# Opening of a transformer block: square sums on VectorE, wide row products, another order of products, zero products

## Chip, cores and metric

One core of a Trainium2 chip (trn2) runs the kernel; the other cores are idle. The metric is device time in microseconds (us) from one launch to its end; lower is better. Three runs of the kernel before took 1899.18, 1899.2 and 1902.77 us, median 1899.2.

## What is computed

One layer on 256 tokens of width 2048, all in float32: a feed-forward half step, attention of two kinds, a second feed-forward half step. Only the first lines matter here:

```
mod = silu(c) @ w_ada + b_ada                      # 9 vectors of 2048: shift, scale, gate, three times
sh1, sc1, gt1, sh2, sc2, gt2, sh3, sc3, gt3 = split(mod)
n   = modulate(rms_norm(h, g_ffn1), sh1, sc1)       # n * (1 + sc1) + sh1
f   = (silu(n @ w1_gate) * (n @ w1_up)) @ w1_down
h   = h + 0.5 * gt1 * f
```

`rms_norm` divides each token by the root of its mean square over the 2048 features.

## The kernel before

The features lie on the partitions: `h` is 16 tiles (`k` from 0 to 15) of 128 features x 256 tokens. A float32 product is made of three fast ones: the weights are split into a high half (`hiw`, cast by ScalarE, L84) and a low half (`low`, raw minus high, VectorE, L91), the normed tile into `nh` and its remainder `nl` (both in the tile `nx`); `mm3` (L225 to L227) adds `nh` by high, `nh` by low and `nl` by high. `Flow` streams the weights in units of 128x1024: `fetch` issues a load on SyncE's queue as soon as a low half has freed a raw buffer (4 of them), `to_hi` and `to_lo` make the halves, with 4 and 3 buffers, and `step` does so some units ahead of TensorE and also runs the jobs that make the shift, scale and gate vectors.

Such a vector entry is a row of 2048 weights times silu(c), summed. `cb` is silu(c) spread over all partitions (TensorE makes it with the matrix of ones into four banks `pc`, ScalarE copies it, L584). `ada_use` (L189) makes 128 entries at once on VectorE in two halves of 1024 columns (L198), each a multiply with a running sum and a read of the sum; the first half starts from a bias, the second from the first.

The opening, in the order written:

- SyncE loads the vectors, `x` in four quarters, two halves of the scale weights of k-tile 0, the shift weights of k-tile 0 (`wz`), then by turns two weight units and the scale and shift weights of k-tile 1 and of k-tile 2.
- TensorE is kept at work with products of zeros (`keep_busy`, L554; the zeros are tile 15 of `nx`): six at first, two after each of the first three quarters.
- For each quarter of `x`, ScalarE squares it (L583), VectorE adds the upper half of the features' tiles to the lower (L587), and TensorE sums over the partitions with two products with ones (L589) into `pstat`.
- The shift entries of k-tile 0 are made on TensorE instead of VectorE, as 16 products with one column, each in two passes (`pm`, L595). VectorE adds the bias (L601).
- `rstd_enter` turns `pstat` into the inverse root (`r1`) with one Newton step, and the scaled tile 0 (`g1`).
- `up_start` (L421) then runs over the first three k-tiles. `before1` (L610) prepares each: the four row halves on VectorE (scale, then shift; for k-tile 0 they are there already), the scaled tile (L321), `nh` on ScalarE (L324), high and low halves, `nl` (L327). For each k-tile there are 24 products of 512 columns, for two groups `G` of 4 banks, 12 each. They are called block 0, 1 and 2 here. All 8 banks (`pa`) hold their sums over the three blocks.
- From then on `up_pass` runs the same three k-tiles for the other groups (bank name `pu`), with units of 12 products, and so on to the end of the feed-forward part.

The order on each engine is the order written. At the end of the first feed-forward part and of the attention, `Stat.finish` (L300) sums the last squares over the partitions, again with zero-cost products of 128 columns (L305) before and behind the last one, 6 and 24, whose result nobody reads.

Of the kernel before, what the change touches and what calls it, by code (L numbers as in the profile page):

```python
# [15 lines left out]
P = 128  # L16
# [23 lines left out]
RATE_H = 0.5  # L40
QKV_ORDER = tuple((0, j, c) for c in range(8) for j in (2, 1)) + tuple(
    (g, j, c) for g in range(4) for j in (2, 1, 0) for c in range(8) if g or j == 0)
LOOK = 2
RAWW = 4
RAWA = 3
# [106 lines left out]
def build(tc, a):  # L152
    nc = tc.nc
    with ExitStack() as ctx:
# [5 lines left out]
        def bank(nm):  # L160
            return pb.tile([P, 512], F32, tag="b", name=nm)
# [27 lines left out]
        def ada_use(j, k, b, raw):  # L189
            if j in (1, 4, 7):  # L190
                scale, init = gsc[:, j // 3, k : k + 1], gin[:, j // 3, k : k + 1]
            elif j in (2, 8):
                scale, init = 0.25, gat[:, j // 3 // 2, k : k + 1]
            else:
                scale, init = 0.5, vec[:, BA + j * KT + k : BA + j * KT + k + 1]
            if b == 1:
                init = acc[:, j, k : k + 1]
            nc.vector.tensor_tensor_reduce(  # L198
                out=raw, in0=raw, in1=cb[:, b * CW : (b + 1) * CW], scale=scale, scalar=init,
                op0=ALU.mult, op1=ALU.add, accum_out=acc[:, j, k : k + 1])  # L200
            if b == 1:
                modded.add((j, k))
# [21 lines left out]
        def mm3(out, lh, ll, rh, rl, first, last, **kw):  # L224
            nc.tensor.matmul(out, lh, rh, start=first, stop=False, **kw)  # L225
            nc.tensor.matmul(out, lh, rl, start=False, stop=False, **kw)  # L226
            nc.tensor.matmul(out, ll, rh, start=False, stop=last, **kw)  # L227
# [14 lines left out]
        def rstd_tiles(w, tag):  # L242
            ts = [sp.tile([P, S], F32, tag="nt", bufs=4, name="rt")[:, :w] for i in range(2)]
            return ts + [(cp if w == 8 else sp).tile([P, w], F32, tag=tag, bufs=2, name=tag)]
# [13 lines left out]
        def rstd_enter(ps, n, k, jsc):  # L258

            t0, t1, r = ts = rstd_tiles(S, "rs")  # L260
            g = sp.tile([P, S], F32, tag="nt", bufs=4, name="nt")
            rstd_act(ps, n, ts)
            nc.scalar.activation(t0, r, AF.Square)
            nc.vector.tensor_scalar(t1, ps, -0.5 / n, -0.5 * EPS, ALU.mult, ALU.add)
            nc.vector.scalar_tensor_tensor(g, h[k], mod(jsc, k), r, ALU.mult, ALU.mult)
            nc.vector.tensor_tensor(t0, t0, t1, ALU.mult)
            nc.vector.scalar_tensor_tensor(g, t0, 1.5, g, ALU.add, ALU.mult)
            nc.vector.scalar_tensor_tensor(r, t0, 1.5, r, ALU.add, ALU.mult)
            return r, g

        class Stat:
# [28 lines left out]
            def finish(self, busy=None):  # L300
                def keep_busy(n):
                    if busy is not None:
                        idle = bank("idle")
                        for i in range(2 * n):
                            nc.tensor.matmul(idle[:, :P], busy[:, 0, :P], busy[:, 1, :P], start=True, stop=True)  # L305

                self.ps = bank("pstat")[:, :S]
                nc.tensor.matmul(self.ps, ones, self.acc, start=True, stop=False)
                keep_busy(3)
                nc.tensor.matmul(self.ps, ones, self.last, start=False, stop=True)  # L310
                keep_busy(12)
# [3 lines left out]
        def norm_parts(k, r, jsc, jsh, made=None):  # L315
            t = made if made is not None else sp.tile([P, S], F32, tag="nt", bufs=4, name="nt")
            sh = mod(jsh, k)

            def p0():
                if made is None:  # L320
                    nc.vector.scalar_tensor_tensor(t, h[k], mod(jsc, k), r, ALU.mult, ALU.mult)  # L321

            def p1():
                nc.scalar.activation(nh[k], t, AF.Identity, bias=sh)  # L324

            def p2():
                nc.vector.scalar_tensor_tensor(nl[k], t, sh, nh[k].bitcast(F32), ALU.add, ALU.subtract)  # L327
                normed.add(k)

            return p0, p1, p2  # L330
# [23 lines left out]
        def wide3(ps, k, whi, wlo, first, last):  # L354
            assert k in normed, k
            for t in range(2):
                ts_ = slice(t * P, (t + 1) * P)
                mm3(ps[t], nh[k][:, ts_], nl[k][:, ts_], whi, wlo, first, last)

        def keep(hp, G, j, ps):  # L360
            if j == 0:
# [23 lines left out]
        def hid_soon(hp, G, d):  # L385
# [32 lines left out]
            fl.at(d + 3, e2)  # L418
            fl.at(d + 4, e3)

        def up_start(hp, K, before):  # L421
            pa = [[[bank(f"pa{G}") for t in range(2)] for j in range(2)] for G in range(2)]
            for k in range(K):
                for G in range(2):
                    whi, wlo = before(k, G)
                    for j in range(2):
                        sl = slice(j * 512, (j + 1) * 512)
                        wide3(pa[G][j], k, whi[:, sl], wlo[:, sl], k == 0, k == K - 1)
                    if k == K - 1:
                        for j in range(2):  # L430
                            fl.at(0, lambda G=G, j=j: keep(hp, G, j, pa[G][j]))
# [96 lines left out]
        def big(nm):  # L528
            return hp.tile([P, 8, S], F32, tag="hid", name=nm)

        def eighths(nm):
            t = big(nm)
            return [t[:, 4 * b : 4 * b + 4, :].rearrange("p a s -> p (a s)") for b in range(2)]

        nc.sync.dma_start(vec, a["vecs"])
        for q in range(4):
            nc.sync.dma_start(h4[q], a["x"][q])
        zero, early = eighths("wz"), {}
        early[0, 1] = eighths("ra")
        for b in range(2):  # L540
            nc.sync.dma_start(early[0, 1][b], a["w_ada"][KT, b])
        for b in range(2):
            nc.sync.dma_start(zero[b], a["w_zero"][b])
        fl.fetch(1)
        for k in range(1, K1):
            for j in (1, 0):
                early[k, j] = eighths("ra")
                for b in range(2):
                    nc.sync.dma_start(early[k, j][b], a["w_ada"][j * KT + k, b])
            fl.fetch(min(2 * k + 1, RAWW - 1))  # L550

        idle = bank("idle")

        def keep_busy(n):  # L554
            for i in range(n):
                nc.tensor.matmul(
                    idle, nx[KT - 1][:, 0, :P], nx[KT - 1].rearrange("p t s -> p (t s)"), start=True, stop=True)

        cc = vec[:, CC : CC + KT]
        sc2 = cp.tile([P, KT], F32, name="sc2")  # L560
# [18 lines left out]
        for q in range(4):  # L579
            if q % 2 == 0:  # L580
                sq8 = big("sq1")
            sq = sq8[:, 4 * (q % 2) : 4 * (q % 2) + 4, :]
            nc.scalar.activation(sq, h4[q], AF.Square)  # L583
            nc.scalar.copy(cb[:, q * 512 : (q + 1) * 512], pcs[q])  # L584
            if q == 3:
                ada_use(1, 0, 0, early[0, 1][0])
            nc.vector.tensor_tensor(sq[:, 0:2, :], sq[:, 0:2, :], sq[:, 2:4, :], ALU.add)  # L587
            for i in range(2):
                nc.tensor.matmul(ps1, ones, sq[:, i, :], start=q + i == 0, stop=q + i == 4)  # L589
            if q < 3:  # L590
                keep_busy(2)
        ada_use(1, 0, 1, early[0, 1][1])
        pm = bank("pm")
        for c in range(KT):
            nc.tensor.matmul(  # L595
                pm[:, 0:1], zero[c // 8][:, c % 8 * P : (c % 8 + 1) * P], sc2[:, c : c + 1],
                start=c == 0, stop=c == KT - 1)
        r1, g1 = rstd_enter(ps1, D, 0, 1)

        def shift0():  # L600
            nc.vector.tensor_scalar(  # L601
                acc[:, 0, 0:1], pm[:, 0:1], 0.5, vec[:, BA : BA + 1], ALU.mult, ALU.add)

        modded.add((0, 0))

        mod_jobs(range(K1, KT), 1, 0, r1)
        ada_jobs([(j, k) for j in (2, 4, 3, 5) for k in range(KT)])
        mod_jobs(range(SPLIT2[0]), 7, 6)

        def before1(k, j):  # L610
            u = fl.u
            if j == 0:
                if k:
                    for i in (1, 0):
                        for b in range(2):
                            ada_use(i, k, b, early[k, i][b])
                fl.to_hi(u)
                p0, p1, p2 = norm_parts(k, r1, 1, 0, None if k else g1)
                p0()
                if k == 0:  # L620
                    shift0()
                p1()
                fl.to_hi(u + 1)
                fl.to_lo(u)
                p2()
                fl.to_lo(u + 1)
                if k == K1 - 1:
                    fl.top_up()
            if k == K1 - 1:
                return fl.step()  # L630
            fl.u += 1
            return fl.hi.pop(u), fl.lo.pop(u)

        up_start(hp, K1, before1)
        fl.pace(RATE_A)
        up_pass(hp, 2, 0, K1, "first")
        fl.pace(RATE_B)
# [406 lines left out]
```

## Time and profile before

| | us |
|---|---|
| median of 3 runs | 1899.2 |
| lowest, highest run | 1899.18, 1902.77 |
| the profiled execution | 1901.4 |
| its span, from the first to the last instruction | 1899.6 |
| TensorE busy in it | 1889.2 |
| VectorE busy in it | 1519.2 |
| ScalarE busy in it | 907.3 |
| mean share of the granted TensorE clock | 0.997 |

The profiled execution is one more run. All times of rows are us from the start of its span. "PE" is TensorE, "PEld" its weight loads, "DVE" VectorE, "ACT" ScalarE. A row of the timeline has the start, the time, engine, line, operation, `out<-in`, shapes, the count, and in brackets how long the engine was idle before and who released it. Matmuls overlap, so their step from start to start is shorter than the time of one.

### The profile page before, as it was taken

To read this page: it belongs to the slowest core of one execution; us is meant where nothing else is said; L and a number is where in the kernel's file an instruction comes from. 1 tells how busy PE (TensorE), PEld (TensorE's weight loads), DVE (VectorE), ACT (ScalarE), POOL (GpSimd) and SP (SyncE) were. 2 spreads that over 40 slices of the span, in tenths; PEclk is the share of its full clock that TensorE was granted. 3 is DMA by queue.
4 is the path that set the end of the run, shared out by engine and by line. 5 is a ranking of instruction groups with operands and counts; after the bars stand their busy time and mean duration, and the time that the engine had idled before them with its cause. 6 is when DMAs were issued, how large, how long until landed. Compare 5 with 4: busy or idle time off the path is not lost.

```text
span 1899.6 us, 25193 instructions
## 1 busy us (share of the span) xinstructions
PE 1889.2 (99%) x9136; PEld 1590.6 (84%) x9136; DVE 1519.2 (80%) x2058; ACT 907.3 (48%) x1261; POOL 1.2 (0%) x7
## 2 busy tenths in 40 slices
PE   8999999999999999999999999999999999999999
PEld 6888888888888888888888998888888888888888
DVE  7989988888889889788887988777877888866444
ACT  5654444444444443556556554654443544433442
POOL 0000000000000000000000000000000000000000
PEclk8999999999999999999999999999999999999999
DMA  8998987777799999586766546988888666687664
GB/s 343 363 336 309 308 294 251 249 257 248 254 365 359 350 367 351 198 265 231 258 220 225 185 152 221 311 307 277 269 274 266 217 227 217 222 288 244 201 198 132
DMA packets 140813, 503.85 MB, mean 265 GB/s; under 512 B 15632, under 2 KB 17936, under 8 KB 140688
## 3 DMA queue, kind: packets, MB, share of 16 engines
q1 hardware_dynamic: 140688, 502.25, 76.9%
q8 instruction: 71, 1.16, 0.2%
q14 instruction: 54, 0.44, 0.1%
HBM read 500.09 MB, written 2.10 MB: 264 GB/s over the span
## 4 chain that ended last, share of the span: by engine, by line
PE 98%; DVE 1%; issue 0%; ACT 0%; DVEq 0%
PE pu L227 16%; PE pu L226 16%; PE pu L225 16%; PE pd L225 6%; PE pd L227 6%; PE pd L226 6%; PE pd L230 4%; PE pd L231 2%; PE pso L225 2%; PE pso L226 2%; PE pso L227 2%; PE pqk L225 2%; PE pqv L225 2%; PE pqq L225 2%; PE pqk L226 2%; PE pqk L227 2%
## 5 line engine op out<-in xcount | busy, mean ns | idle before, releaser
L84 ACT CAST hiw<-rw 128x1024 fp32r<-128x1024 f32 x656 | 691.4, 1055 | 932.9 <-PE pu L227 441.6
L91 DVE TENSOR_TENSOR low<-rw,hiw 128x1024 fp32r<-128x1024 f32 x656 | 801.7, 1222 | 333.6 <-issue 109.9
L225 PE MATMUL pu<-hiw,nx 128*128 128x512 f32 x1352 | 527.7, 390 | 0.0
L227 PE MATMUL pu<-hiw,nx 128*128 128x512 f32 x1352 | 526.1, 389 | 0.0
L226 PE MATMUL pu<-low,nx 128*128 128x512 f32 x1352 | 526.0, 389 | 0.0
L227 PEld LDWEIGHTS pu<-hiw,nx 128*128 128x128 f32 x1352 | 253.8, 188 | 52.6
L226 PEld LDWEIGHTS pu<-low,nx 128*128 128x128 f32 x1352 | 253.8, 188 | 52.3
L225 PEld LDWEIGHTS pu<-hiw,nx 128*128 128x128 f32 x1352 | 253.8, 188 | 52.0
L225 PE MATMUL pd<-hiw,hd 128*128 128x512 f32 x528 | 205.9, 390 | 0.0
L227 PE MATMUL pd<-hiw,hd 128*128 128x512 f32 x528 | 205.4, 389 | 0.0
L226 PE MATMUL pd<-low,hd 128*128 128x512 f32 x528 | 205.4, 389 | 0.0
L198 DVE CUSTOM_DVE_ANT_0 ra<-ra,cb,acc 128x1024 f32<-128x1024 f32 x143 | 185.6, 1298 | 0.1
L230 PE MATMUL pd<-hd,hiw 128*128 128x512 f32 x336 | 116.9, 392 | 0.0
L227 PEld LDWEIGHTS pd<-hiw,hd 128*128 128x128 f32 x528 | 99.1, 188 | 20.7
L225 PEld LDWEIGHTS pd<-hiw,hd 128*128 128x128 f32 x528 | 99.1, 188 | 20.3
L226 PEld LDWEIGHTS pd<-low,hd 128*128 128x128 f32 x528 | 99.1, 188 | 20.3
L368 DVE TENSOR_TENSOR pt<-pt,pu 128x512 f32<-128x512 f32 x176 | 112.3, 679 | 0.0
L231 PE MATMUL pd<-hd,low 128*128 128x256 f32 x336 | 94.1, 280 | 0.0
L198 DVE CUSTOM_DVE_ANT_0 ra<-ra,cb,vec 128x1024 f32<-128x1024 f32 x63 | 80.5, 1278 | 0.0
L230 PEld LDWEIGHTS pd<-hd,hiw 128*128 128x128 f32 x336 | 62.9, 187 | 13.8
L225 PE MATMUL pso<-ox,hiw 128*128 128x256 f32 x256 | 73.1, 286 | 0.0
L227 PE MATMUL pso<-ox,low 128*128 128x256 f32 x256 | 72.4, 283 | 0.0
(168 smaller groups left out, 2015.0 us busy)
## 6 DMA issues: line engine op xcount, KB each, us to landing
ra<-in_w_ada_dram SPq DMA_DIRECT2D x286, 512.0 KB, 5.0
rw<-in_w_d_dram SPq DMA_DIRECT2D x176, 512.0 KB, 4.6
rw<-in_w_c_dram SPq DMA_DIRECT2D x154, 512.0 KB, 4.3
rw<-in_w_b_dram SPq DMA_DIRECT2D x121, 512.0 KB, 4.7
rw<-in_w_qkv_dram SPq DMA_DIRECT2D x96, 512.0 KB, 4.2
rw<-in_w_a_dram SPq DMA_DIRECT2D x63, 512.0 KB, 5.1
rw<-in_w_o_dram SPq DMA_DIRECT2D x32, 512.0 KB, 3.3
rw<-in_w_s_dram SPq DMA_DIRECT2D x14, 512.0 KB, 3.4
```

What stands on the lines that cost most here:

```text
L84: self.nc.scalar.copy(t, self.raw[self.nhi])
L91: self.nc.vector.tensor_tensor(t, self.raw.pop(self.nlo), self.hi[self.nlo].bitcast(F32), ALU.subtract)
L198: nc.vector.tensor_tensor_reduce(out=raw, in0=raw, in1=cb[:, b * CW : (b + 1) * CW], scale=scale, scalar=init, op0=ALU.mult, op1=ALU.add, ...
L225: nc.tensor.matmul(out, lh, rh, start=first, stop=False, **kw)
L226: nc.tensor.matmul(out, lh, rl, start=False, stop=False, **kw)
L227: nc.tensor.matmul(out, ll, rh, start=False, stop=last, **kw)
L230: nc.tensor.matmul(ps, lh, r.rearrange("p t s -> p (t s)"), start=first, stop=False)
L231: nc.tensor.matmul(ps[:, :S], ll, r[:, 0, :], start=False, stop=last)
L368: nc.vector.tensor_tensor(part[G][:, j, t, :], part[G][:, j, t, :], ps[t], ALU.add)
```

## The change

- **Squares**: after the first addition VectorE adds the two remaining tiles as well, and TensorE makes one product with ones for each quarter instead of two; the zero products between the quarters go. ScalarE's copies to `cb` come one quarter later.
- **Tile 0**: VectorE makes the scaled tile without the scale entry (`hr`), ScalarE adds the bias of the shift entries, and makes `nh` and once more the same in full precision (`tt`); VectorE subtracts. The cast of the second weight unit stands behind these.
- **Rows of k-tiles 1 and 2**: one product over 2048 columns (`row_use`) in place of two over 1024, with the scaled tile between the scale row and the shift row. `nl` is made ahead of the two low halves.
- **Blocks**: `wide6` takes each group's 12 products by kind: four on `nh` and the high half, four on `nl` and the high half, four on `nh` and the low half.
- **Zero products**: six ahead of block 1 and twelve ahead of block 2, of 512 columns, added as zeros to the first bank.
- **`Stat.finish`**: 3 and 12 zero-cost products of 512 columns in place of 6 and 24 of 128.

```diff
+GAPS = (6, 12)
...
                 def keep_busy(n):
                     if busy is not None:
                         idle = bank("idle")
-                        for i in range(2 * n):
-                            nc.tensor.matmul(idle[:, :P], busy[:, 0, :P], busy[:, 1, :P], start=True, stop=True)
+                        for i in range(n):
+                            nc.tensor.matmul(
+                                idle, busy[:, 0, :P], busy.rearrange("p t s -> p (t s)"), start=True, stop=True)
...
+        def wide6(pa, k, whi, wlo, first, last):
+
+            assert k in normed, k
+            for w, x in ((whi, nh[k]), (whi, nl[k]), (wlo, nh[k])):
+                for j in range(2):
+                    for t in range(2):
+                        nc.tensor.matmul(
+                            pa[j][t], x[:, t * P : (t + 1) * P], w[:, j * 512 : (j + 1) * 512],
+                            start=first and w is whi and x is nh[k], stop=last and w is wlo)
...
+        blank = nx[KT - 1].rearrange("p t s -> p (t s)")
+
+        def keep_busy(n, out=idle, first=True):
+
             for i in range(n):
-                nc.tensor.matmul(
-                    idle, nx[KT - 1][:, 0, :P], nx[KT - 1].rearrange("p t s -> p (t s)"), start=True, stop=True)
+                nc.tensor.matmul(out, blank[:, :P], blank, start=first, stop=first)
...
             nc.scalar.activation(sq, h4[q], AF.Square)
-            nc.scalar.copy(cb[:, q * 512 : (q + 1) * 512], pcs[q])
+            for c in ((), (0,), (1,), (2, 3))[q]:
+                nc.scalar.copy(cb[:, c * 512 : (c + 1) * 512], pcs[c])
             if q == 3:
-                ada_use(1, 0, 0, early[0, 1][0])
+                ada_use(1, 0, 0, early[1, 0][:, :CW])
             nc.vector.tensor_tensor(sq[:, 0:2, :], sq[:, 0:2, :], sq[:, 2:4, :], ALU.add)
-            for i in range(2):
-                nc.tensor.matmul(ps1, ones, sq[:, i, :], start=q + i == 0, stop=q + i == 4)
-            if q < 3:
-                keep_busy(2)
-        ada_use(1, 0, 1, early[0, 1][1])
+            nc.vector.tensor_tensor(sq[:, 0, :], sq[:, 0, :], sq[:, 1, :], ALU.add)
+            nc.tensor.matmul(ps1, ones, sq[:, 0, :], start=q == 0, stop=q == 3)
+        ada_use(1, 0, 1, early[1, 0][:, CW:])
...
-        r1, g1 = rstd_enter(ps1, D, 0, 1)
-
-        def shift0():
-            nc.vector.tensor_scalar(
-                acc[:, 0, 0:1], pm[:, 0:1], 0.5, vec[:, BA : BA + 1], ALU.mult, ALU.add)
-
+        t0, t1, r1 = ts1 = rstd_tiles(S, "rs")
+        hr, tt = [sp.tile([P, S], F32, tag="nt", bufs=4, name="nt") for i in range(2)]
+        rstd_act(ps1, D, ts1)
+        nc.scalar.activation(t0, r1, AF.Square)
+        nc.vector.tensor_scalar(t1, ps1, -0.5 / D, -0.5 * EPS, ALU.mult, ALU.add)
+        nc.vector.tensor_tensor(t0, t0, t1, ALU.mult)
+        nc.vector.scalar_tensor_tensor(r1, t0, 1.5, r1, ALU.add, ALU.mult)
+        nc.vector.tensor_tensor(hr, h[0], r1, ALU.mult)
+        fl.to_hi(0)
+        nc.scalar.activation(acc[:, 0, 0:1], pm[:, 0:1], AF.Identity, scale=0.5, bias=vec[:, BA : BA + 1])
         modded.add((0, 0))
+        nc.scalar.activation(nh[0], hr, AF.Identity, scale=mod(1, 0), bias=mod(0, 0))
+        nc.scalar.activation(tt, hr, AF.Identity, scale=mod(1, 0), bias=mod(0, 0))
+        fl.to_hi(1)
+        fl.to_lo(0)
+        nc.vector.tensor_tensor(nl[0], tt, nh[0].bitcast(F32), ALU.subtract)
+        fl.to_lo(1)
+        normed.add(0)
...
+        def row_use(j, k):
+            nc.vector.tensor_tensor_reduce(
+                out=early[j, k], in0=early[j, k], in1=cb,
+                scale=gsc[:, 0, k : k + 1] if j else 0.5,
+                scalar=gin[:, 0, k : k + 1] if j else vec[:, BA + k : BA + k + 1],
+                op0=ALU.mult, op1=ALU.add, accum_out=acc[:, j, k : k + 1])
+            modded.add((j, k))
...
+        pa = [four(G) for G in range(2)]
+        for G in range(2):
+            wide6(pa[G], 0, *own(), True, False)
+        for k in range(1, K1):
             u = fl.u
...
+            row_use(1, k)
+            t = sp.tile([P, S], F32, tag="nt", bufs=4, name="nt")
+            nc.vector.scalar_tensor_tensor(t, h[k], mod(1, k), r1, ALU.mult, ALU.mult)
+            row_use(0, k)
+            _, p1, p2 = norm_parts(k, r1, 1, 0, t)
+            fl.to_hi(u)
+            p1()
+            fl.to_hi(u + 1)
+            p2()
+            fl.to_lo(u + 1)
+            if k == K1 - 1:
+                fl.top_up()
+            keep_busy(GAPS[k - 1], pa[0][0][0], False)
+            for G in range(2):
+                w = own() if k < K1 - 1 else fl.step()
+                wide6(pa[G], k, *w, False, k == K1 - 1)
```

`own()` hands out the next unit's halves without making new ones; `four(G)` takes four banks. The loads on SyncE's queue keep their order.

The order shows it at three places. On TensorE, around the squares, before (`pc` spreads silu(c), `pstat` sums squares, `idle` takes the zero products, `pm` the shift entries):

```order
L571 MATMUL pc<-dg,ones 128x512 x4
L589 MATMUL pstat<-sq_171,ones 128x256 x2
L556 MATMUL idle<-nx_97 128x512 x2
L589 MATMUL pstat<-sq_171,ones 128x256 x2
L556 MATMUL idle<-nx_97 128x512 x2
L589 MATMUL pstat<-sq_186,ones 128x256 x2
L556 MATMUL idle<-nx_97 128x512 x2
L589 MATMUL pstat<-sq_186,ones 128x256 x2
L595 MATMUL pm<-sc_140,wz 128x1 x16
```

and in the changed kernel:

```order
L591 MATMUL pc<-dg,ones 128x512 x4
L610 MATMUL pstat<-sq_171,ones 128x256 x2
L610 MATMUL pstat<-sq_181,ones 128x256 x2
L614 MATMUL pm<-sc_140,wz 128x1 x16
L368 MATMUL pa_240<-hiw,nx_82 128x512
```

Of eight products with ones and six with zeros, four with ones are left between `pc` and `pm`.

On VectorE, from the second low half of block 0 to block 1's remainder (`ra` holds a row's weights, `acc` the entries, ISA with `acc` alone reads a sum), before:

```order
L91 TENSOR_TENSOR low<-rw,hiw 128x1024
L198 ISA ra,acc<-ra,cb,gin,gsc 128x1024
L198 ISA acc 128x1
L198 ISA ra,acc<-ra,cb,acc,gsc 128x1024
L198 ISA acc 128x1
L198 ISA ra,acc<-ra,cb,vec 128x1024
L198 ISA acc 128x1
L198 ISA ra,acc<-ra,cb,acc 128x1024
L198 ISA acc 128x1
L321 SCALAR_TENSOR_TENSOR nt<-h_78,acc,rs 128x256
L91 TENSOR_TENSOR low<-rw,hiw 128x1024
L327 SCALAR_TENSOR_TENSOR nx_83<-nt,acc,nx_83 128x256
```

and in the changed kernel:

```order
L92 TENSOR_TENSOR low<-rw,hiw 128x1024
L641 ISA ra,acc<-ra,cb,gin,gsc 128x2048
L641 ISA acc 128x1
L659 SCALAR_TENSOR_TENSOR nt<-h_78,acc,rs 128x256
L641 ISA ra,acc<-ra,cb,vec 128x2048
L641 ISA acc 128x1
L329 SCALAR_TENSOR_TENSOR nx_83<-nt,acc,nx_83 128x256
L92 TENSOR_TENSOR low<-rw,hiw 128x1024 x2
```

Two products stand for four, the scaled tile `nt` moved between them, and the remainder (`nx_83`) ahead of both low halves.

On TensorE, from block 0 to block 1 (`nx_82` is k-tile 0, `nx_83` k-tile 1; a bank of `pa` has its number), before:

```order
L225 MATMUL pa_237<-hiw,nx_82 128x512
L226 MATMUL pa_237<-low,nx_82 128x512
L227 MATMUL pa_237<-hiw,nx_82 128x512
L225 MATMUL pa_230<-hiw,nx_83 128x512
L226 MATMUL pa_230<-low,nx_83 128x512
L227 MATMUL pa_230<-hiw,nx_83 128x512
```

and in the changed kernel:

```order
L368 MATMUL pa_246<-low,nx_82 128x512
L368 MATMUL pa_247<-low,nx_82 128x512
L577 MATMUL pa_240<-nx_97 128x512 x6
L368 MATMUL pa_240<-hiw,nx_83 128x512
L368 MATMUL pa_241<-hiw,nx_83 128x512
L368 MATMUL pa_242<-hiw,nx_83 128x512
L368 MATMUL pa_243<-hiw,nx_83 128x512
L368 MATMUL pa_240<-hiw,nx_83 128x512
```

The low half moved from the second product of a block to the ninth, and six zero products stand between the blocks.

## Rows read from the trace of the kernel before

**Rows 1.** The page: busy us of each engine, and the chain of waits.

```profile
PE 1889.2 (99%) x9136; PEld 1590.6 (84%) x9136; DVE 1519.2 (80%) x2058; ACT 907.3 (48%) x1261; POOL 1.2 (0%) x7
...
PE 98%; DVE 1%; issue 0%; ACT 0%; DVEq 0%
```

**Rows 2.** Windows: stretch, length, busy (count) of PE, PEld, DVE, ACT, POOL, clock, DMA.

```profile
8.80:13.00 4.20, 4.12 (x19) 3.19 (x17) 2.63 (x5) 2.65 (x4) 0.00 (x0) 1.00 1.02 418
14.40:16.40 2.00, 2.00 (x20) 2.00 (x20) 1.59 (x4) 1.62 (x4) 0.00 (x0) 1.00 1.03 422
16.50:18.50 2.00, 2.00 (x11) 2.00 (x11) 0.37 (x2) 0.48 (x1) 0.00 (x0) 0.50 1.02 418
19.60:23.20 3.60, 3.60 (x8) 2.70 (x9) 3.56 (x6) 0.87 (x1) 0.00 (x0) 0.50 1.03 421
...
37.00:40.30 3.30, 3.30 (x8) 2.60 (x9) 2.51 (x3) 2.01 (x3) 0.00 (x0) 0.50 0.63 207
```

**Rows 3.** Timeline of TensorE, pm and the three blocks.

```profile
14.04 4.69 PE L595 MATMUL pm<-sc,wz 128*128 128x1 f32 x32
19.59 0.80 PE L225 MATMUL pa<-hiw,nx 128*128 128x512 f32 x1 [0.85 <-ACT nx L324]
...
26.46 0.39 PE L226 MATMUL pa<-low,nx 128*128 128x512 f32 x1
26.69 0.39 PE L227 MATMUL pa<-hiw,nx 128*128 128x512 f32 x1
27.91 0.49 PE L225 MATMUL pa<-hiw,nx 128*128 128x512 f32 x1 [0.83 <-ACT nx L324]
...
36.23 0.51 PE L225 MATMUL pa<-hiw,nx 128*128 128x512 f32 x1 [2.03 <-ACT nx L324]
...
37.41 0.63 PE L227 MATMUL pa<-hiw,nx 128*128 128x512 f32 x1
37.83 0.63 PE L225 MATMUL pa<-hiw,nx 128*128 128x512 f32 x1
...
43.78 0.39 PE L225 MATMUL pu<-hiw,nx 128*128 128x512 f32 x1
```

**Rows 4.** Groups by line and shape, VectorE, first 60 us (busy, mean ns, idle).

```profile
L91 DVE TENSOR_TENSOR low<-rw,hiw 128x1024 fp32r<-128x1024 f32 x14 | 17.0, 1222 | 5.3 <-issue 2.1 <-ACT pt L364 1.5 <-PE pu L226 1.5
...
L587 DVE TENSOR_TENSOR sq<-sq 128x512 f32<-128x512 f32 x4 | 2.8, 692 | 2.0 <-ACT sq L583 2.0
```

**Rows 5.** Timeline of VectorE, from pm's end to the rows of k-tile 2.

```profile
18.77 0.22 DVE L601 TENSOR_SCALAR acc<-pm,vec 128x1 f32<-128x1 f32 x1 [1.90 <-PE pm L595]
...
20.50 1.23 DVE L91 TENSOR_TENSOR low<-rw,hiw 128x1024 fp32r<-128x1024 f32 x1
21.64 1.34 DVE L198 CUSTOM_DVE_ANT_0 ra<-ra,cb,gin 128x1024 f32<-128x1024 f32 x1
...
26.83 0.48 DVE L321 SCALAR_TENSOR_TENSOR nt<-h,acc,rs 128x256 f32<-128x256 f32 x1
27.23 1.22 DVE L91 TENSOR_TENSOR low<-rw,hiw 128x1024 fp32r<-128x1024 f32 x1
...
29.96 1.34 DVE L198 CUSTOM_DVE_ANT_0 ra<-ra,cb,gin 128x1024 f32<-128x1024 f32 x1
```

**Rows 6.** Timeline of ScalarE behind pm.

```profile
19.02 0.51 ACT L324 ACTIVATE nx<-nt,acc 128x256 fp32r<-128x256 f32 x1 [2.04 <-DVE acc L601]
19.44 1.03 ACT L84 CAST hiw<-rw 128x1024 fp32r<-128x1024 f32 x1
```

**Rows 7.** Timelines of VectorE and TensorE at the first `Stat.finish`.

```profile
760.08 0.43 DVE L282 TENSOR_TENSOR sq<-h 128x256 f32<-128x256 f32 x1
...
760.91 2.98 PE L305 MATMUL idle<-hd 128*128 128x128 f32 x24
764.18 0.50 PE L225 MATMUL pqv<-hiw,nx 128*128 128x512 f32 x1 [0.30 <-ACT nx L324]
```

**Rows 8.** Timeline of ScalarE in the pass after the blocks.

```profile
48.12 1.06 ACT L84 CAST hiw<-rw 128x1024 fp32r<-128x1024 f32 x1 [0.98 <-DMA rw<-in_w_a_dram]
```

More of the change, by code (lines that the diff above doesn't have):

```diff
@@ L419, in hid_soon, with four @@
             fl.at(d + 4, e3)
+        def four(G):
+            return [[bank(f"pa{G}") for t in range(2)] for j in range(2)]
         def up_start(hp, K, before):
-            pa = [[[bank(f"pa{G}") for t in range(2)] for j in range(2)] for G in range(2)]
+            pa = [four(G) for G in range(2)]
             for k in range(K):
@@ L533, in eighths, with whole, row_load @@
             return [t[:, 4 * b : 4 * b + 4, :].rearrange("p a s -> p (a s)") for b in range(2)]
+        def whole(nm):
+            return big(nm).rearrange("p a s -> p (a s)")
+        def row_load(t, j, k):
+            for b in range(2):
+                nc.sync.dma_start(t[:, b * CW : (b + 1) * CW], a["w_ada"][j * KT + k, b])
         nc.sync.dma_start(vec, a["vecs"])
@@ L537, in build @@
             nc.sync.dma_start(h4[q], a["x"][q])
[L538 to L541, printed above, removed]
+        zero, early = eighths("wz"), {(1, 0): whole("ra")}
+        row_load(early[1, 0], 1, 0)
         for b in range(2):
@@ L546, in build @@
             for j in (1, 0):
-                early[k, j] = eighths("ra")
-                for b in range(2):
-                    nc.sync.dma_start(early[k, j][b], a["w_ada"][j * KT + k, b])
+                early[j, k] = whole("ra")
+                row_load(early[j, k], j, k)
             fl.fetch(min(2 * k + 1, RAWW - 1))
         idle = bank("idle")
-        def keep_busy(n):
+        blank = nx[KT - 1].rearrange("p t s -> p (t s)")
+        def keep_busy(n, out=idle, first=True):
             for i in range(n):
-                nc.tensor.matmul(
-                    idle, nx[KT - 1][:, 0, :P], nx[KT - 1].rearrange("p t s -> p (t s)"), start=True, stop=True)
+                nc.tensor.matmul(out, blank[:, :P], blank, start=first, stop=first)
         cc = vec[:, CC : CC + KT]
@@ L608, in build, with own @@
         mod_jobs(range(SPLIT2[0]), 7, 6)
-        def before1(k, j):
-            u = fl.u
[L612 to L626, printed above, removed]
-                if k == K1 - 1:
[L628 to L634, printed above, removed]
+        def row_use(j, k):
[5 more added lines that the diff above has]
+            modded.add((j, k))
+        def own():
+            fl.u += 1
+            return fl.hi.pop(fl.u - 1), fl.lo.pop(fl.u - 1)
+        pa = [four(G) for G in range(2)]
+        for G in range(2):
+            wide6(pa[G], 0, *own(), True, False)
+        for k in range(1, K1):
+            u = fl.u
+            row_use(1, k)
[14 more added lines that the diff above has]
+                wide6(pa[G], k, *w, False, k == K1 - 1)
+                if k == K1 - 1:
+                    for j in range(2):
+                        fl.at(0, lambda G=G, j=j: keep(hp, G, j, pa[G][j]))
         fl.pace(RATE_A)
```

## The prediction

> **What bounds the kernel now.** I read the page's busy table and its chain of waits first. TensorE is busy for 99% of the span and the chain is TensorE for 98% [rows 1], so the time is the length of TensorE's queue, and a change can win only what TensorE loses. The next view is the list of windows of the first 44 us [rows 2], because the diff lies there but for two later spots, and then TensorE's timeline of the same stretch [rows 3]. The reader is to see three kinds of loss.
>
> First, gaps. The shift column's 32 one-column passes (pm) end at 14.04 + 4.69 = 18.73; I call that moment X. Block 0 (k-tile 0, 24 products) starts at 19.59, block 1 at 27.91 (X + 9.18) and block 2 at 36.23 (X + 17.50); the last two waited 0.83 and 2.03 us for ScalarE's nx [rows 3].
>
> Second, the clock. The records give 2.4 GHz (1.00) up to 16.4, 1.2 GHz (0.50) from 16.5 to 23.2, and 1.2 GHz once more from 37.0 to 40.3 [rows 2]. It fell once while TensorE ran only pm, although the busy column says 2.00 of 2.00 there, and once after the 2.03 us gap. A 512-column product is 0.23 us apart at the high level (26.46 to 26.69) and 0.42 at the low one (37.41 to 37.83) [rows 3].
>
> Third, order. In block 0 and block 1 the second and third products wait for the low half and the remainder, which VectorE makes last. Block 2 therefore needs 43.78 - 36.23 = 7.55 us, against 24 x 0.227 = 5.45 for 24 products without a stall at 2.4 GHz. From 43.78 on TensorE does not stop again until the end of the first feed-forward part, so what is won before 43.78 is won at the end.
>
> **The change part by part.** I sum everything up to the moment at which the products of the next pass begin, 43.78 before.
>
> *Squares.* The 6 zero products between the quarters go, and a second addition halves the ones-products. The added addition of 256 columns is half as wide as the one of 0.69 us [rows 4], so about 0.4, and it lies on the path of the last quarter only; against it half of that quarter's products goes. Ends: -0.3, were the addition hidden, and +0.4, were the products free; I take +0.1, since the two are of one size. The sum of squares itself is not urgent: VectorE had done all that hangs on it and waited 1.90 us for pm [rows 5].
>
> But the zero products were also what kept TensorE working from 9 to 13 us at 2.4 GHz [rows 2]. Without them it does three pairs of passes in some 5 us, so I take the clock to be low when pm begins. pm ran 20 passes in 2.00 us at 2.4 GHz and 11 in 2.00 us at 1.2 GHz [rows 2], hardly anything else being in these stretches: 0.10 and 0.18 us each. All 32 at the low level take 5.8, against the 4.69 of the mixed row [rows 3]: **+1.1**. The ends are 32 x 0.10 = 3.2 (-1.5) and 5.8; I take the upper, because in the only stretch where TensorE did little but pm the clock fell. So X moves from 18.73 to 19.9. The bank of pm and both halves of its weights are there earlier, nothing else waits.
>
> What the Trainium skill says of this (TensorE: Matmul & The Clock Gate, section "What's actually happening") is that the slow clock is the default and activity of TensorE releases it, so a run of matmuls without a gap should bring it back. The row speaks against that for pm: the clock fell inside it. By the Trainium skill pm would be mixed again and the sum below would be 1.1 us lower; by the row it stays.
>
> *Tile 0.* The shift column goes from VectorE (0.22 [rows 5]) to ScalarE, at the same place behind pm; no cost. ScalarE then makes nh as before (19.02, X + 0.29), but a second such product (tt, taken as 0.42 by the step from 19.02 to 19.44) comes ahead of the weight cast that stood at 19.44 [rows 6]. So the cast and the second low half on VectorE, 20.50 before [rows 5], come 0.4 later: VectorE starts on the rows of k-tile 1 at X + 3.3, where it was X + 2.9 (21.64).
>
> *Products over 2048 columns.* Four halves took 26.83 - 21.64 = 5.19 [rows 5]. An addition of 512 columns takes 0.692 and of 1024 columns 1.222 [rows 4], so 1024 more columns cost 1.06. A row of 2048 then takes 1.34 + 1.06 = 2.40 and with its read some 2.45 or, with a constant scale, 2.38: 4.83 for both, 0.36 less per tile. Ends: no gain (twice the 1.34) and 0.5. I take 0.36, the value that the widths give.
>
> *Remainders last.* The scaled tile now stands between the two row products, and the remainder of x follows ScalarE's nh at once, ahead of both low halves. Before, the first low half ran while ScalarE made nh; now VectorE waits that time out, about 0.7 later at the second tile's rows than before. Chain: X + 3.3 + 4.83 + 0.40 (the scaled tile, 26.83 to 27.23 [rows 5]) = X + 8.5, and 0.68 more by nh to the first product (27.23 to 27.91): block 1 can start at X + 9.2 (before 9.18). The remainder starts when nh is there, some 0.1 ahead of the block, and takes 0.48, two low halves 1.14 each (20.50 to 21.64): rows at X + 11.9 (before 29.96, X + 11.23), tile at X + 17.1, block 2 at X + 17.8: **+0.3** over the X + 17.50 of before. So VectorE's gain is spent.
>
> *Order within a block.* Four products on nh and the high half come first, then four on the remainder, then four on the low half. Remainder and low half are due 0.9 and 1.8 us after the block's start, and by the chain above they come 0.4 and 1.5 after it. No stall is left.
>
> *Zero products.* Six and twelve of 0.227 each: 1.4 and 2.7 us. Block 0 starts at X + 0.84; at the low level for 3.7 us as before (19.59 to 23.2 and a little) it does 8.7 products, the other 15.3 take 3.5: it ends at X + 8.0, with the zeros at X + 9.4, 0.2 past block 1's operands. Block 1 ends at X + 14.9, with its zeros X + 17.6, before X + 17.8. So the first six cost nothing that lasts, and the twelve hold the clock: block 2 takes 5.45 for 7.55, **-2.1**.
>
> *The two later spots.* 30 short zero products become 15 of 512 columns. The second group took 2.98 and becomes 12 x 0.227 = 2.7; TensorE waits 0.30 for nx behind it, and nx hangs on the sum of squares, whose last square VectorE makes up to 760.5 [rows 7]; the first group, 6 short ones or 3 x 0.227, is over by then. Cost 0. They may hold the clock in an execution where the short ones do not: down to -2.1 each by the price of block 2, but both stretches were at 2.4 GHz in this trace, so 0.
>
> *Later loads.* The fifth low half now ends near X + 19.3 = 39.2; before, block 2 had used it by 37.4 [rows 3], so it is 1.8 later at least and I take 2.5. The next weight tile leaves behind it. A cast waited 0.98 for such a tile at 48.12 [rows 8], while TensorE came to it at 43.78 + 4 x 2.72 = 54.7: a lead of 5.5 us with the cast's own time, of which some 3 go. Cost 0 while that lead lasts.
>
> Sum: 0.1 + 1.1 + 0.3 - 2.1, that is **-0.6** against the profiled execution of 1901.4 (span 1899.6 and 1.8 around it): 1900.8. The median of the runs shown, 1899.2, lies 2.2 lower, and the runs reach from 1899.18 to 1902.77. If the 2.2 is constant, the changed kernel takes 1898.6; if the median's runs had no slow stretch in block 2, that term is theirs already and 1900.8 stands. I take the middle, **1899.7**.
>
> **The rivals.**
> 1. *The clock holds into pm, or comes back in it.* For it: TensorE's busy column is full there. Against: it fell there. X as before or up to 1.5 earlier; sum -1.7 to -3.2, so 1897.5 to 1896.0 on the median's level. 17%. (The rule of the Trainium skill named above points this way.)
> 2. *The zeros turn on the path* (slower). They stand behind block 0 whatever the time is, and decide as soon as block 0 ends later than X + 7.8. Should the clock stay at 1.2 GHz through all of block 0, it ends at 20.7 + 24 x 0.427 = 31.0, zeros 32.3, block 1 37.8, zeros 40.5, block 2 45.9: +2.2, 1901.4 on the median's level and 1903.6 on the profile's. For it: pm leaves the clock low for longer. Against: 3.6 us of products sufficed before. 8%.
> 3. *A row of 2048 costs two of 1024.* Block 2 0.7 later: sum +0.1, no change, 1899.3 to 1901.5. Against: the widths of the additions. 10%.
> 4. *The weights come late in the pass after 44 us*, because the lead is shorter and the queue near its best rate there. Up to +2 us on the sum, 1900.6 to 1902.8. Against: the lead of 5.5. 5%.
>
> **How the numbers follow.** The forecast has 60%. The range 1896.8 to 1902.8 takes in rivals 1, 3 and 4 and half of 2. 0.2% is 3.8 us, about what a measurement of this kernel can tell from no change: faster means under 1895.4, which needs all of rival 1 and a fast draw, 5%; slower means over 1903.0, rival 2 at the profile's level, 4%; the rest, 91%, is no change.
>
> **What would show it.** pm at 1.2 GHz with X near 19.9; row products of 2.4; block 1 and 2 starting at X + 9.4 and X + 17.8; no low clock after block 0; the next pass beginning near 43.2. Wrong would be X under 18.7, a block 0 at 1.2 GHz to its end, or a wait of TensorE for weights after 44 us.

## The result, and the profile after

| | before | changed |
|---|---|---|
| median, us | 1900.70 (22 runs) | 1903.26 (22 runs) |
| lowest, highest | 1899.16, 1902.77 | 1900.38, 1903.61 |
| ratio to before | | 1.0013, 95% interval 1.0007 to 1.0019 |

The change costs 2.6 us, 0.13%. By the bound of 0.2% that is no change, as was held likeliest; but the interval of the ratio leaves out 1, so the small loss is clear of noise, and the time lies 0.5 above the range's upper end of 1902.8. The median of before moved too, from 1899.2 with 3 runs to 1900.7 with 22.

The profiled execution of the changed kernel took 1900.38 and is the fastest of its 22. Its page:

```profile
span 1898.6 us, 25142 instructions
...
PE 1890.1 (100%) x9110; PEld 1591.4 (84%) x9110; DVE 1519.6 (80%) x2052; ACT 908.0 (48%) x1263; POOL 1.2 (0%) x7
```

VectorE's 1519.6 stands against 1519.2 in [rows 1]: in sum nothing is saved there. TensorE is busy to 100%, and the span is 1.0 shorter than before, though the median is 2.6 longer. So one execution does not stand for this kernel, and the second view has to be of another one. TensorE's timeline of the first profile:

```profile
13.09 5.29 PE L614 MATMUL pm<-sc,wz 128*128 128x1 f32 x32
19.36 3.78 PE L368 MATMUL pa<-hiw,nx 128*128 128x512 f32 x8 [0.98 <-ACT nx L628]
...
28.93 1.98 PE L368 MATMUL pa<-hiw,nx 128*128 128x512 f32 x8
...
37.09 1.98 PE L368 MATMUL pa<-hiw,nx 128*128 128x512 f32 x8
...
42.62 0.50 PE L226 MATMUL pu<-hiw,nx 128*128 128x512 f32 x1
```

and of e4 below, the changed kernel but for the two later sums, in an execution of 1903.55, where most runs of the changed kernel lie too:

```profile
13.56 1.19 PE L609 MATMUL pstat<-sq,ones 128*128 128x256 f32 x2 [2.10 <-DVE sq L608]
14.54 6.83 PE L613 MATMUL pm<-sc,wz 128*128 128x1 f32 x32
22.35 3.72 PE L367 MATMUL pa<-hiw,nx 128*128 128x512 f32 x8 [0.98 <-ACT nx L627]
...
29.55 1.52 PE L576 MATMUL pa<-nx 128*128 128x512 f32 x6
30.91 1.98 PE L367 MATMUL pa<-hiw,nx 128*128 128x512 f32 x8
...
36.35 2.88 PE L576 MATMUL pa<-nx 128*128 128x512 f32 x12
39.16 2.11 PE L367 MATMUL pa<-hiw,nx 128*128 128x512 f32 x8
...
45.77 0.50 PE L226 MATMUL pu<-hiw,nx 128*128 128x512 f32 x1 [0.88 <-ACT pt L375]
```

Against [rows 3] three things are to be seen. pm takes 6.83 instead of 4.69 and ends at X = 21.37 instead of 18.73. Blocks 1 and 2 start without a wait, behind the zeros. And a wait of 0.88 that was not there stands ahead of the next pass, which begins at 45.77 instead of 43.78. In the first profile the clock fell at 14.8, when pm had run for 1.7 us, X was 18.38, and the wait was absent.

Everything behind these 46 us is the same within 0.15 us. In each profiled execution I took the moment at which the next pass begins, and the time from there to the first product of the attention (`pqv`), of the second feed-forward part (`pa`) and to the end:

| profile | next pass | to pqv | to pa | to the end |
|---|---|---|---|---|
| before | 43.78 | 720.40 | 399.99 | 735.43 |
| changed | 42.62 | 720.54 | 400.01 | 735.43 |
| e1, changed again | 44.27 | 720.54 | 400.01 | 735.38 |
| e4 | 45.77 | 720.55 | 400.02 | 735.46 |

The time is decided in the first 46 us. The two later spots of the change are in the other columns: "to pqv" is 0.14 longer in the changed kernel, and as long in e4, which has the old sums; the rest did not move.

### The profile page after: what moved, and what is told of

It is laid out like the page before. It is cut to its first block, busy times and chain, and to the rows that moved or that the text cites. A ratio compares the mean times of both kernels' runs of the same rounds, so it can differ in the third digit from the quotient of the medians.

```text
span 1898.6 us, 25142 instructions
## 1 busy us (share of the span) xinstructions
PE 1890.1 (100%) x9110; PEld 1591.4 (84%) x9110; DVE 1519.6 (80%) x2052; ACT 908.0 (48%) x1263; POOL 1.2 (0%) x7
## 4 chain that ended last, share of the span: by engine, by line
PE 99%; DVE 0%; DMA 0%; ACT 0%; SPq 0%; issue 0%; DVEq 0%
PE pu L226 16%; PE pu L228 16%; PE pu L227 16%; PE pd L228 6%; PE pd L226 6%; PE pd L227 6%; PE pd L231 4%; PE pd L232 2%; PE pso L226 2%; PE pso L227 2%; PE pso L228 2%; PE pqv L226 2%; PE pqk L226 2%; PE pqq L226 2%; PE pqk L227 2%; PE pqq L227 2%
## 5 line engine op out<-in xcount | busy, mean ns | idle before, releaser
L199 DVE CUSTOM_DVE_ANT_0 ra<-ra,cb,acc 128x1024 f32<-128x1024 f32 x139 | 180.5, 1299 | 0.0
L226 PE MATMUL pso<-ox,hiw 128*128 128x256 f32 x256 | 73.2, 286 | 0.0
L227 PE MATMUL pso<-ox,hiw 128*128 128x256 f32 x256 | 72.5, 283 | 0.0
```

The lines of the kernel that those rows point to most:

```text
L199: nc.vector.tensor_tensor_reduce(out=raw, in0=raw, in1=cb[:, b * CW : (b + 1) * CW], scale=scale, scalar=init, op0=ALU.mult, op1=ALU.add, ...
```

## The experiments

**e1: the changed kernel once more.** 

> The changed kernel once more, for a second profiled execution: the first took 1900.4, while the median of its 22 runs is 1903.3. Theory A (the clock comes back late): in an execution near 1903 all of block 0 and part of the zero products run at 1.2 GHz, the next pass begins at 45 us or later instead of 42.6, and TensorE waits for no weights. Theory B (weights late): the next pass begins near 43, and TensorE then waits for high or low halves between 45 and 70 us, 2 to 3 us in all. Theory C (the two later sums): the difference lies at about 760 and 1160 us, as a stretch at 1.2 GHz or a longer wait there. Time 1902 to 1904 for all three.

Median 1902.83 of 10 runs, ratio 1.0013 (1.0004 to 1.0023); the profiled execution took 1902.02. pm began at 13.19 and took 6.54, so X = 19.73, the next pass at 44.27, with a wait of 1.00 for the banks ahead of it; no wait for weights after 44 us and nothing at 760 and 1160 us. Theories B and C fall. Of A the place is right, the picture wrong: block 0 ran at 1.2 GHz for some 3 us only, as in the kernel before. What came later was pm.

**e2: no zero products ahead of blocks 1 and 2.**

```diff
-            keep_busy(GAPS[k - 1], pa[0][0][0], False)
```

> The six and twelve zero products ahead of blocks 1 and 2 left out. Theory A: the products were on the path behind a late block 0; without them 1 to 2.5 us less than the changed kernel where the clock holds, at most 1.7 back where it falls in the gap before block 2: 1901 to 1902.5. Theory B and C: the weights and the later sums are as late as before, 1902.5 to 1905.

Median 1903.59, ratio 1.0017 (1.0008 to 1.0027): not faster, 0.8 above e1 on the same chip. So those zeros are not what costs, and theory A in this form falls. Its profile, the fastest of its runs, shows one thing more:

```profile
38.72 2.11 PE L368 MATMUL pa<-hiw,nx 128*128 128x512 f32 x8 [2.71 <-ACT nx L326]
```

TensorE waited 2.71 us ahead of block 2 without any product of zeros, and the eight products behind the wait took 2.11, as in e4 (39.16): the granted clock was 1.00 through the wait and the block. So it is not shown that the twelve zeros are what keeps block 2 at 2.4 GHz.

**e3: two zero products again behind each of the first three quarters.**

```diff
             nc.tensor.matmul(ps1, ones, sq[:, 0, :], start=q == 0, stop=q == 3)
+            if q < 3:
+                keep_busy(2)
```

> Two zero products again behind each of the first three quarters of the squares, as in the kernel before. Theory A: the clock is still at 2.4 GHz when pm begins, pm takes 4.7 instead of 5.3 to 5.8 and ends 0.6 to 1.1 earlier: 1901.5 to 1903. Theory B: a pm that ends earlier changes nothing in the lead of the weights: 1902.5 to 1903.5. Theory C: 1902.3 to 1903.3.

Median 1900.03, ratio 1.0000 (0.9991 to 1.0009), 2.8 under e1 on the same chip and beyond what any theory gave. TensorE's timeline of e3:

```profile
13.38 0.67 PE L610 MATMUL pstat<-sq,ones 128*128 128x256 f32 x2 [1.61 <-DVE sq L609]
13.89 4.43 PE L616 MATMUL pm<-sc,wz 128*128 128x1 f32 x32
...
42.80 0.50 PE L226 MATMUL pu<-hiw,nx 128*128 128x512 f32 x1 [0.85 <-ACT pt L376]
```

Against e4 the last quarter's passes take 0.67 instead of 1.19 and pm 4.43 instead of 6.83. Six products whose result nobody reads give back the whole loss, by the medians.

**e4: the two later sums as before.**

```diff
-                        for i in range(n):
-                            nc.tensor.matmul(
-                                idle, busy[:, 0, :P], busy.rearrange("p t s -> p (t s)"), start=True, stop=True)
+                        for i in range(2 * n):
+                            nc.tensor.matmul(idle[:, :P], busy[:, 0, :P], busy[:, 1, :P], start=True, stop=True)
```

> The two later sums with 6 and 24 short zero products of 128 columns, as in the kernel before; the rest as changed. Theory C: back by 2 to 3 us, 1900 to 1901.5. Theories A and B: as the changed kernel, 1902.5 to 1903.6.

Median 1903.23, ratio 1.0013 (1.0004 to 1.0022): the later sums cost and give nothing. Its profile shows the clock of the loss, in windows:

```profile
12.50:13.50 1.00, 0.00 (x0) 0.00 (x0) 0.96 (x3) 0.00 (x0) 0.00 (x0) 0.50 1.03 422
14.60:21.40 6.80, 6.77 (x33) 6.68 (x31) 2.90 (x7) 2.24 (x4) 0.00 (x0) 0.50 1.03 420
22.40:25.40 3.00, 3.00 (x7) 2.44 (x8) 2.06 (x3) 2.28 (x3) 0.00 (x0) 0.50 1.02 419
26.00:45.00 19.00, 18.89 (x83) 15.04 (x81) 16.94 (x18) 6.58 (x8) 0.00 (x0) 1.00 0.57 201
```

TensorE is idle and at 1.2 GHz before the last quarter arrives, and stays there through all of pm, busy for 6.77 of 6.80 us. The last row is all of blocks 1 and 2 with the zeros between: full clock.

The wait ahead of the next pass is explained by ScalarE's timeline of e4:

```profile
44.18 1.05 ACT L85 CAST hiw<-rw 128x1024 fp32r<-128x1024 f32 x1 [2.23 <-DMA rw<-in_w_a_dram]
45.14 2.04 ACT L375 COPY pt<-pa 128x512 f32<-128x512 f32 x4
```

ScalarE waits 2.23 us for a weight unit that TensorE needs only two units later, and the copies that free the banks for the next pass are queued behind that cast.

**e5: the kernel before once more**, unedited. 

> The kernel before once more, for a second profiled execution; its runs lie in two groups, 1899.2 and 1900.4 to 1901.4, and the first profile was of 1901.4. Theory P (all that differs between executions lies ahead of the next pass): the stretch from the next pass to the end is again 1855.8 us, and an execution near 1899.2 starts that pass at 41.6, without the slow stretch in block 2; one near 1901 starts it at 43.5. Rival: the start stays at 43.8 and the rest is shorter.

1900.65, next pass at 42.97, the rest 720.40, 400.01 and 735.42. Block 2 began at 35.72 and ran partly at 1.2 GHz here as well. The rest is constant, as theory P said; an execution near 1899.2 was not caught, so it is not shown that it lacks the slow stretch of block 2.

**e6: the kernel before without the six zero products in the squares.**

```diff
-            if q < 3:
-                keep_busy(2)
```

> The kernel before with nothing changed but the six zero products between the quarters of the squares left out. Theory P: pm runs at 1.2 GHz to its end, 6.8 us for 4.7, X moves from 18.7 to 20.8 to 21.4 and the whole chain with it: 1902 to 1903.5. Rival Q (the loss comes from the further addition on VectorE and the path over ScalarE for tile 0): no change, 1899.2 to 1901.

Median 1900.23, ratio 0.9999 (0.9990 to 1.0008): no loss. My theory of the zeros alone was wrong. The timeline shows why:

```profile
8.04 3.14 PE L589 MATMUL pstat<-sq,ones 128*128 128x256 f32 x12
12.48 1.13 PE L589 MATMUL pstat<-sq,ones 128*128 128x256 f32 x4 [1.30 <-DVE sq L587]
13.45 5.49 PE L593 MATMUL pm<-sc,wz 128*128 128x1 f32 x32
```

and so does a window around pm's start, whose granted clock, 1.00, stands in the last column but two:

```profile
13.10:14.10 1.00, 1.00 (x10) 0.95 (x8) 0.60 (x2) 0.45 (x1) 0.00 (x0) 1.00 1.04 426
```

The two products of each of the first three quarters fill 3.14 us with passes by themselves, and pm still begins at the high clock: 5.49 in this execution, not 6.83. One execution would not decide it, since the first profile of the changed kernel has 5.29; the median does.

**e9: the changed kernel with two products with ones for each quarter**, so without the second addition, and without zeros.

```diff
-            nc.vector.tensor_tensor(sq[:, 0, :], sq[:, 0, :], sq[:, 1, :], ALU.add)
-            nc.tensor.matmul(ps1, ones, sq[:, 0, :], start=q == 0, stop=q == 3)
+            for i in range(2):
+                nc.tensor.matmul(ps1, ones, sq[:, i, :], start=q + i == 0, stop=q + i == 4)
```

> The changed kernel with the second addition undone, so two products with ones for each quarter, and no zero products between them. Theory P2 (in the squares TensorE has too little work only when both go, the zeros and half of the products with ones; e6 lost the zeros alone and was not slower): pm begins at 2.4 GHz as in e6 and takes 4.7 to 5.6, 1899.5 to 1901. Rival T (the zeros alone decide in the changed kernel, whose block order or tile 0 differs): as the changed kernel, 1902.5 to 1903.5.

Median 1901.25, ratio 1.0004 (0.9995 to 1.0013), 0.25 above the stretch given, pm 5.21. It lies 1.15 above the 1900.1 of before in the same comparison, so somewhat more than half of the 2.6 is gone by undoing the addition alone; where the rest lies was not followed up.

**e10: the kernel before with the second addition and without the zeros**, nothing else of the change.

```diff
-            for i in range(2):
-                nc.tensor.matmul(ps1, ones, sq[:, i, :], start=q + i == 0, stop=q + i == 4)
-            if q < 3:
-                keep_busy(2)
+            nc.vector.tensor_tensor(sq[:, 0, :], sq[:, 0, :], sq[:, 1, :], ALU.add)
+            nc.tensor.matmul(ps1, ones, sq[:, 0, :], start=q == 0, stop=q == 3)
```

> The kernel before with the second addition and without the zeros between the quarters, nothing else of the change. Theory P2: pm at 1.2 GHz from its first pass in most executions, 6.8 us, X at 20.8 to 21.4, the rest of the chain behind it: 1902 to 1903.8. Rival T: as e6, 1899.5 to 1901.

Median 1903.49, ratio 1.0017 (1.0008 to 1.0025), 3.4 above the 1900.1 of before: this one part of the change costs as much by itself as the whole change, or more. Its timeline has the same pm, and a window shows the clock low from pm's start (0.50):

```profile
12.98 1.19 PE L589 MATMUL pstat<-sq,ones 128*128 128x256 f32 x2 [1.66 <-DVE sq L588]
13.97 6.83 PE L593 MATMUL pm<-sc,wz 128*128 128x1 f32 x32
```

```profile
13.10:14.10 1.00, 1.00 (x4) 0.82 (x4) 1.00 (x2) 0.00 (x0) 0.00 (x0) 0.50 1.01 414
```

Rival T falls: taking out the zeros alone (e6) or adding the additions alone (e3) costs nothing; the time is lost when both kinds of TensorE's work are gone. The moment at which the clock falls says the same: in the six profiles without both kinds (the first one, e1, e2, e4, e10, e12) it falls between 12.2 and 14.8 us, in the eight that keep one or both (before, e3, e5 to e9, e11) between 14.9 and 18.0. The two groups nearly touch, so a single profile of either kind can mislead.

**e12: the changed kernel with the copies ahead of the cast on ScalarE.**

```diff
-                        fl.at(0, lambda G=G, j=j: keep(hp, G, j, pa[G][j]))
+                        fl.at(0, lambda G=G, j=j: keep(hp, G, j, pa[G][j]), -1)
```

> The changed kernel with the copies out of block 2's banks ahead of the cast on ScalarE, nothing else. Theory P: TensorE's wait of 0.9 to 1.0 for the first bank goes in the executions that have it: 1901.9 to 1902.6, against 1902.8 to 1903.3 for the changed kernel. Rival R (another wait takes its place): 1902.7 to 1903.4.

Median 1901.96, ratio 1.0010 (1.0001 to 1.0018), 1.3 under the changed kernel's 1903.26 and 0.9 under e1's 1902.83, in other comparisons. In its profile pm takes 6.82 and the next pass begins without a wait, 5.44 behind block 2's start (38.94 to 44.38). The wait was worth about 1 us; the intervals of the two ratios overlap, so this rests on the wait that is gone from the profile, with the medians agreeing.

**e7: e3 with the copies ahead of the cast** (both edits above). 

> The changed kernel with two zero products behind each of three quarters, as e3, and with the copies out of block 2's banks ahead of the cast of the ninth weight unit on ScalarE. Theory P: TensorE's wait of 0.85 for the banks goes, the next pass starts at 41.9 instead of 42.8: 0.6 to 0.9 under e3, 1899.0 to 1899.6. Rival R (the bank's wait hides another, of the weights behind it): no gain over e3, 1899.8 to 1900.3.

Median 1899.52, ratio 0.9995 (0.9986 to 1.0004), 0.5 under e3; the next pass begins at 41.70, with no wait. With both losses mended, what is left of the change is worth about 1 us, and that is not clear of the measurement.

**e8: e7 with the weights of pm loaded first.**

```diff
-        row_load(early[1, 0], 1, 0)
         for b in range(2):
             nc.sync.dma_start(zero[b], a["w_zero"][b])
+        row_load(early[1, 0], 1, 0)
...
         nc.vector.tensor_scalar(t1, ps1, -0.5 / D, -0.5 * EPS, ALU.mult, ALU.add)
+        ada_use(1, 0, 0, early[1, 0][:, :CW])
...
         nc.vector.tensor_tensor(hr, h[0], r1, ALU.mult)
+        ada_use(1, 0, 1, early[1, 0][:, CW:])
```

(with the two old calls of `ada_use` taken out). 

> e7, and the weights of pm loaded ahead of the scale row of tile 0, whose two halves VectorE now makes behind the squares. Theory P (X sets all that follows): pm starts near 11.5 and ends near 15.5, tile 0 is then bound by VectorE near 16.5, the next pass starts near 39.9: 1897 to 1898.2. Rival S (the rows of k-tiles 1 and 2 then wait for their loads): 1898.2 to 1899.6.

Median 1898.82, ratio 0.9991 (0.9982 to 1.0000): above theory P's 1897 to 1898.2, in the stretch of rival S. The waits for loads that rival S names do not show in the profile, where VectorE's rows follow one another without one; what the other executions lose stays open. pm begins at 11.79 and ends at 15.57; block 0 begins at 17.46 and now waits for VectorE's second half of the scale row. The next pass begins at 40.06 in a profile of 1897.97, the fastest of its runs.

**e11: e8 with three and ten zero products** (`GAPS = (3, 10)`). 

> e8 with three and ten zero products ahead of blocks 1 and 2 instead of six and twelve. In e8 both blocks began right behind the zeros, while nx was there 0.3 us earlier for block 2. Theory Z (with an early X the zeros themselves are on the path): 0.3 to 1 us under e8, 1897.8 to 1898.5. Rival (the gaps left open let the clock fall in block 2 in some executions): 1898.8 to 1900.

Median 1898.14 of 11 runs (1897.79 to 1898.81), ratio 0.9990 (0.9981 to 0.9999): 2.4 under before, and the narrowest spread of all. Over e8 that is 0.7 in another comparison, and the two ratios differ by 0.0001, so the gain from fewer zeros is not clear of noise. TensorE's timeline of its profiled execution, the slowest of its runs:

```profile
12.86 3.63 PE L613 MATMUL pm<-sc,wz 128*128 128x1 f32 x32
18.52 3.44 PE L368 MATMUL pa<-hiw,nx 128*128 128x512 f32 x8 [2.03 <-ACT nx L629]
...
26.88 2.11 PE L368 MATMUL pa<-hiw,nx 128*128 128x512 f32 x8 [0.58 <-ACT nx L326]
...
35.33 2.11 PE L368 MATMUL pa<-hiw,nx 128*128 128x512 f32 x8 [0.43 <-ACT nx L326]
...
40.90 0.39 PE L226 MATMUL pu<-hiw,nx 128*128 128x512 f32 x1
```

Blocks 1 and 2 wait 0.58 and 0.43 for nx and no longer stand behind zeros, as theory Z wanted. All of pm is at 2.4 GHz, 3.63 us.

## Why the prediction was right and where it was wrong

The frame held: the time is won or lost before the next pass begins, and hardly anything behind it moved. So did most terms, in e4's execution, counted from X:

| step | predicted | e4 |
|---|---|---|
| row product of 2048 columns | 2.40 | 2.41 |
| end of block 0's products | X + 8.0 | X + 8.18 |
| block 1 | X + 9.4 | X + 9.54 |
| block 2 | X + 17.8 | X + 17.79 |
| block 2's length | 5.45 | 5.44 (e12) |
| the two later spots | 0 | 0 |
| X | 19.9 | 21.37 |
| wait ahead of the next pass | 0 | 0.88 |

The row products are these, on VectorE in e4, with the scaled tile between them:

```profile
24.90 2.41 DVE L640 CUSTOM_DVE_ANT_0 ra<-ra,cb,gin 128x2048 f32<-128x2048 f32 x1
27.23 0.09 DVE L640 DVE_READ_ACCUMULATOR2_ANT acc<- 128x1 f32 x1
27.35 0.48 DVE L658 SCALAR_TENSOR_TENSOR nt<-h,acc,rs 128x256 f32<-128x256 f32 x1
27.76 2.34 DVE L640 CUSTOM_DVE_ANT_0 ra<-ra,cb,vec 128x2048 f32<-128x2048 f32 x1
```

One agreement is not the mechanism's merit. Block 2's gain was put down to the twelve zeros that hold the clock; e2 has no zeros there and ran block 2 at 2.4 GHz too, so the size came out and the reason given is not shown. In some executions the zeros may help: e2's median is 0.8 above e1's, though the intervals of the two ratios overlap.

**The step that failed is "Squares".** Its mechanism was right and was named: with so little work for TensorE in the squares pm runs at 1.2 GHz, to its end in e4 and for all but its first 0.3 us in e1. Both of its terms were mis-sized. pm was put at 5.8, from 11 passes in a window of 2.00 us [rows 2]; it takes 6.83, that is 0.213 a pass. A window's count takes in passes that began before it, and a pass lasts longer than the step from one to the next (0.35 on average in e4), so 2.00/11 is too short a step. The start and end of the whole group would have been the right row. And the second addition was set at +0.1, because fewer products with ones stand behind it. This is the last quarter's first addition in the profile of before, on VectorE:

```profile
12.34 0.69 DVE L587 TENSOR_TENSOR sq<-sq 128x512 f32<-128x512 f32 x1
```

and in e4:

```profile
12.27 0.69 DVE L607 TENSOR_TENSOR sq<-sq 128x512 f32<-128x512 f32 x1
```

From here to pm it took 1.70 in before and 2.27 in e4, where the two passes at 1.2 GHz take 1.19, about what four took at 2.4 GHz (1.13): +0.6. In the first profile and in e1 the two passes ran at 2.4 GHz and the way took 1.80, so there +0.1 was right. Their pm began earlier than in before, at 13.09 and 13.19, only because that first addition did, at 11.29 and 11.39. In e4 X moved by 2.64 instead of 1.2.

**The second miss is "Later loads", cost 0.** The lead of the weights over TensorE was counted, and rightly, since no product waited for weights. What was left out is what stands behind the waiting cast in ScalarE's queue: the copies that free the banks. The later low half, foreseen as 2.5 us, became 0.88 of TensorE's wait; e12 took it away.

Put together, in e4 against the profile of before: X +2.64, block 2 behind X +0.29, from block 2 to the next pass -0.94 (6.61 for 7.55, the wait of 0.88 included), sum +1.99 = 45.77 - 43.78. The prediction had +1.2, +0.3 and -2.1.

**The rivals.** Rival 1, the clock coming back inside pm, was wrong: e4's pm ran 6.8 us without a gap at 1.2 GHz. That also goes against the rule of the Trainium skill that was weighed there (TensorE: Matmul & The Clock Gate, section "What's actually happening"): TensorE was busy for 6.77 of 6.80 us, and the clock did not come back. Rival 2, the zeros on the path, was wrong in its size: block 0 came back to 2.4 GHz as foreseen, and the six zeros cost 0.2 to 0.3 for block 1 (X + 9.54, and X + 9.34 without them in e2) that block 2 does not see (X + 17.79 in both). With an early X, in e8, blocks 1 and 2 start right behind the zeros, 0.7 and 0.4 after nx is there; that this costs time is not clear from e11's median. Rival 3 is excluded by the 2.41. Rival 4 was right in that a load comes late, and wrong about who waits.

Put into the prediction's own sum, pm's 6.83 (+1.0), the addition (+0.5) and the wait (+0.9) turn -0.6 into +1.8, so 1903.2 over the profiled 1901.4, against 1903.26 measured. The forecast lay another 1.1 lower, because the middle was taken between the sum's 1900.8 and the level of a median of three runs, 1899.2; with 22 runs that median is 1900.7. The range rested on the same three runs and on a pm that could not exceed 5.8.

## What to carry to other kernels

Before filler work or surplus products are removed from a faster engine's queue, see what runs next at the clock that they kept up: here six products with zeros and four with ones less ahead of a short group made that group up to 2.1 us longer, and only the removal of both kinds of work did it. When an engine is to wait longer for a load that nobody needs yet, look at what is queued behind that wait, not at the load's own lead. And where executions of one kernel differ by more than the effect, find the one moment that carries the spread before profiles are compared.

## What the runs showed of the hardware beyond what was expected

A group of 32 one-column passes with a weight load each took 3.63 us at 2.4 GHz (e11) and 6.83 at 1.2 GHz (e4, e10): it scales with the clock nearly in full, 0.113 and 0.213 a pass, though hardly a column is streamed. In e4 and e10 the clock did not come back inside such a group, and in before, the first profile and e1 it fell inside one, while TensorE was busy. Products of zeros behind the squares kept it at 2.4 GHz for longer: in e3 it fell at 16.5, in the first profile, e1 and e4 at 14.8, 13.5 and 12.2. For the zeros ahead of blocks 1 and 2 the like is not shown: e4 is at 2.4 GHz from 26 to 45 us over 18 of them, and so is e2 without them, behind a wait of 2.71 us, whereas in before it fell at 36.9 behind one of 2.03 [rows 3]. The moments of falling and rising differ from execution to execution, and with them X: 18.38, 19.73 and 21.37 in the first profile, e1 and e4.
